# A hybrid encoder step on one core: the b gates formed in the order of the merge, and each output row's sigmoid held behind the last piece of gate a

## The chip, the cores and the metric

The kernel runs on one core of a Trainium2 chip. The metric is the time of one execution on the device in microseconds (us), the median of several runs; lower is better. Beside the runs stands one execution recorded by the hardware profiler. Its views give busy times, waits, transfers and the granted clock of TensorE. In them PE is TensorE, DVE is VectorE, ACT is ScalarE, POOL is GpSimd and SP is SyncE; a q behind the name (SPq, POOLq) is that engine's queue of instructions and DMA issues. "L905" is line 905 of the kernel.

## The reference

One layer of an encoder for 1024 prompt frames and 64 frames of a running stream (1088 in all), D_MODEL = 1024, 8 heads of 64, convolution width 512. Everything is float32. Only the mixer bears on this case:

```python
def mixer(xn, conv_prefix, attn_fn, w_in, w_conv, w_conv_out, w_attn_out, w_out):
    proj = xn @ w_in
    cb, cc, ch, q, k, v, ga, gb = jnp.split(proj, splits, axis=-1)
    cv, conv_state = causal_conv(cc * ch, conv_prefix, w_conv)
    ya = (cb * cv) @ w_conv_out
    o, new_k, new_v = attn_fn(heads(q), heads(k), heads(v))
    yb = o.reshape(B, L, ATT_DIM) @ w_attn_out
    merged = jax.nn.sigmoid(ga) * ya + jax.nn.sigmoid(gb) * yb
    return merged @ w_out, conv_state, new_k, new_v
```

A RMSNorm stands ahead of it, and a residual, a SwiGLU network with a second RMSNorm and a last RMSNorm behind it.

## The kernel before

Arrays lie with channels on the 128 partitions and the 1088 frames along a row, so the 1024 channels of a gate are eight row blocks, m = 0 to 7. A float32 product is made of three matmuls on two-part operands (a rounded "hi" part and the rest, "lo"): `split` writes hi with a cast on ACT (L128) and lo with a subtraction on DVE (L129). A gate's row block is formed by `gate` in four pieces of 272 frames; a piece is 24 matmuls (L343 to L345) into one of three PSUM buffers (`pmm`, `bufs=3`), and what reads the piece out frees the buffer.

Ahead of the part that matters lies the convolution branch, whose result `y_d` (for blocks 0 to 5 already times the sigmoid of gate a) waits in DRAM. Then come ten gate blocks, `GATES`: gate b for m = 0 to 7 as i = 0 to 7, and gate a for m = 6 and 7 as i = 8 and 9. Attention, head after head, is interleaved with them. A piece of gate b is copied out of PSUM by ACT (L908, tile `gst`) and stored by POOL to `gb_d` (L909). A piece of gate a (the last two blocks, `LAST = 2`) is not stored: ACT takes its sigmoid straight out of PSUM into `ga` (L905).

Before gate block 8 attention ends. Its output goes through DRAM: `co` tiles (and `co_s` for the 64 stream frames) are stored to `o_d` by SP (L985, L989), and the reciprocals of the softmax sums (`rows`) are stored to `rc_d` by POOL (L1040, L1044). Heads 0 to 3 come back early (`o0`, `o1`). Those of heads 4 to 7 are read by SP after the last stores: the reciprocals into `rc2` and `rc3` (L1090), and o itself into the tile `ob` (L1170, two loads, called ob k=2 and ob k=3 below). DVE multiplies them (L1172), and `split` writes the pair `ob` (the ACT casts `ob<-o0`, `ob<-o1`, `ob<-rc2`, `ob<-rc3`).

The merge goes over the row blocks in the order `MERGE = [6, 7, 0, 1, 2, 3, 4, 5]`. `rows_in(m)` loads the gate b row from `gb_d` into `z`, named `gb0` to `gb7` (L1138), and the y row into `t`, named `yg0` to `yg7` (L1139); it is called for four blocks before gate block 8 and for the others in the loop. The loop takes z's sigmoid on ACT (L1194), forms `yb` = W_attn_out · o on PE, multiplies by z (L1208), adds to t (L1209) and splits into the operand `mg` of the next product, W_out. `wp10` to `wp17` are the parts of W_attn_out's blocks; their casts and subtractions stand between the others, and their loads (`rawp`, L309) and those of W_out (`wor`, L1233) are issued by POOL.

Each engine works through its own instructions in order; SP's and POOL's DMA issues too. That order is set when the program is built, by a scheduler that orders by data dependences and expected readiness: an instruction that stands late in the source can be placed early on its engine. `tc.issue_after(x)` keeps what is written under it behind instruction x.

Of the kernel before, what the change touches and what calls it, by code (L numbers as in the profile page):

```python
# [10 lines left out]
AF = mybir.ActivationFunctionType  # L11
# [55 lines left out]
def encoder_kernel(ctx: ExitStack, tc: tile.TileContext, ins, outs):  # L67
    nc = tc.nc
    mm = nc.tensor.matmul
    vec, act, pool_e = nc.vector, nc.scalar, nc.gpsimd  # L70
# [55 lines left out]
    def split(hi, lo, src):  # L126

        a = act.copy(hi, src)  # L128
        b = vec.tensor_tensor(lo, src, hi.bitcast(F32), op=ALU.subtract)  # L129
        return a.ins, b.ins  # L130
# [71 lines left out]
    class Unit:  # L202
# [20 lines left out]
        def prep(self, step):  # L223

            a11, a12, a21, a22 = self.block(0, 0), self.block(0, 1), self.block(1, 0), self.block(1, 1)

            def sum(o, x, y, op=ALU.subtract):
                vec.tensor_tensor(o, x, y, op=op)

            if step == 0:  # L230
                self.plain(1, a11)
            elif step == 1:
                self.plain(2, a12)
            elif step == "sums":
                self.s1 = self.temp()
                sum(self.s1, a21, a22, ALU.add)
                self.s2 = self.temp()
                sum(self.s2, self.s1, a11)
                sum(a21, a11, a21)
            elif step == 2:  # L240
                if self.s1 is None:
                    self.prep("sums")
                self.plain(6, self.s2)
            elif step == 3:
                self.plain(7, a21)
            elif step == 4:
                self.plain(5, self.s1)
            elif step == 5:
                self.plain(4, a22)
            else:  # L250
                sum(a12, a12, self.s2)
                self.plain(3, a12)
# [77 lines left out]
    def next_w():  # L330
        i = used[0]
        used[0] += 1
        prep(4 if i == 3 else i + 2)
        return plan[i]

    def product(out, w, x, o, n):

        kt = 4 * len(w)
        for k in range(kt):
            a, b = (t[:, k % 4] for t in w[k // 4])  # L340
            p, q = x.at(0, k, o, n), x.at(1, k, o, n)
            first, then = (q, p) if x is xn and o // HN % 2 == 0 else (p, q)
            mm(out, a, first, start=k == 0, stop=False)  # L343
            mm(out, a, then, start=False, stop=False)  # L344
            newest[0] = mm(out, b, p, start=False, stop=k == kt - 1).ins  # L345

    PIECES = [(j * HN, HN) for j in range(4)]
    GATES = [("b", m) for m in range(8)] + [("a", m) for m in range(6, 8)]
    for g, m in GATES:
        if m % 2 == 0:  # L350
            base = (C_GA if g == "a" else C_GB) + m * P
            ld = {"src": w_in[:, base : base + 2 * P], "w": 2 * P}
        plan.append((ld, KD, m % 2 * P))
    MERGE = [6, 7, 0, 1, 2, 3, 4, 5]
    for m in MERGE[::2]:
        ld = {"src": ins["w_attn_out"][0][:, m * P : (m + 2) * P], "w": 2 * P, "at": 40}
        plan += [(ld, 4, j * P) for j in range(2)]
# [540 lines left out]
    def gate(i, cs):  # L898
        g, m = GATES[i]
        for c in cs:  # L900
            o, n = PIECES[c]
            ps = pmm.tile([P, 512], F32, tag="mm", name=f"g{i}_{c}")
            product(ps[:, :n], gate_w[i], xn, o, n)
            if i >= len(GATES) - LAST:
                act.activation(ga_rows[m - 6][:, o : o + n], ps[:, :n], AF.Sigmoid)  # L905
                continue
            st = st_pool.tile([P, HN], F32, tag="st", name=f"gst{i}_{c}")
            act.copy(st[:, :n], ps[:, :n])  # L908
            nc.gpsimd.dma_start(gb_d[m * P : (m + 1) * P, o : o + n], st[:, :n])  # L909

    gate_w = {}

    heads, sums = {}, {}

# [169 lines left out]
    def row_tile(l, nm):  # L1084
        return qp.tile([P, T], F32, tag=f"q{l}", name=nm, bufs=2 + l)
# [42 lines left out]
    def between():  # L1128
        credit[0] += PER
        while credit[0] >= 1:  # L1130
            credit[0] -= 1
            next(steps, None)
# [3 lines left out]
    def rows_in(m):  # L1136
        t, z = rows[m] = u_rows.tile([P, T], F32, tag="yg", name=f"yg{m}"), row_tile((MERGE.index(m) % 5 + 1) % 2, f"gb{m}")
        nc.sync.dma_start(z, gb_d[m * P : (m + 1) * P])  # L1138
        nc.sync.dma_start(t, y_d[m * P : (m + 1) * P])  # L1139
# [4 lines left out]
    for i in range(4):  # L1144
        gate_w[i] = next_w()
        gate(i, (0, 1))
    for i in range(4):
        for c in (2, 3):
            gate(i, (c,))
            between()  # L1150
        if i == 0:
            prep(5)
    for i in range(4, len(GATES)):
        gate_w[i] = next_w()
        if i == len(GATES) - LAST:
            for _ in steps:
                pass
            att_stack.close()
            uo = pg_stack.enter_context(tc.tile_pool(name="uo", bufs=1, reuse_waits="tile"))
            uo.tile([P, 48], F32, name="pad_ob")  # L1160
            t = uo.tile([P, 2, 4 * T + 8], F32R, name="ob")[:, :, : 4 * T]
            ob = Acts(t.rearrange("p l (k t) -> p l k t", k=4))
            u_rows = pg_stack.enter_context(tc.tile_pool(name="u_rows", bufs=5, reuse_waits="tile"))
            ga_rows = [uo.tile([P, T], F32, name=f"ga{m}") for m in (6, 7)]
            for k in range(2):
                split(ob.t[:, 0, k], ob.t[:, 1, k], o_rows[k])
            late_r = row_tile(1, "rc2"), row_tile(0, "rc3")
            for k, r in zip((2, 3), late_r):
                o = ob.t[:, 0, k].bitcast(F32)
                nc.sync.dma_start(o, o_d[k * P : (k + 1) * P])  # L1170
                rc_load(r, k)
                vec.tensor_tensor(r, o, r, op=ALU.mult)  # L1172
                split(ob.t[:, 0, k], ob.t[:, 1, k], r)
            for m in MERGE[:4]:
                rows_in(m)
        for c in range(4):
            gate(i, (c,))
            between()
        if i >= len(GATES) - LAST:
            m = GATES[i][1]  # L1180
            t = rows[m][0]
            vec.tensor_tensor(t, t, ga_rows[m - 6], op=ALU.mult)
# [5 lines left out]
    psum2 = pg_stack.enter_context(tc.tile_pool(name="psum2", bufs=2, space=PSUM, reuse_waits="tile"))  # L1188
    for n, m in enumerate(MERGE):
        wb = next_w()  # L1190
        if n + 4 < 8:
            rows_in(MERGE[n + 4])
        t, z = rows.pop(m)
        act.activation(z, z, AF.Sigmoid)  # L1194
        late = t.rearrange("p (h n) -> p h n", h=2)[:, :, 512:]
        hi, lo = (ms[:, m, l].rearrange("p (h n) -> p h n", h=2) for l in range(2))
        for h in range(2):
            yb = psum2.tile([P, 2, 512], F32, tag="mm", name=f"yb{m}_{h}")
            for j in range(2):
                if n == 0:  # L1200
                    with tc.issue_after(gates_end):
                        product(yb[:, j, :HN], wb, ob, h * HT + j * HN, HN)
                else:
                    product(yb[:, j, :HN], wb, ob, h * HT + j * HN, HN)
            hs = slice(h * HT, (h + 1) * HT)
            zh, th = z[:, hs], t[:, hs]
            two = zh.rearrange("p (j n) -> p j n", j=2)
            vec.tensor_tensor(two, yb[:, :, :HN], two, op=ALU.mult)  # L1208
            vec.tensor_tensor(th, th, zh, op=ALU.add)  # L1209
            split(mg.at(0, m, h * HT, HT), mg.at(1, m, h * HT, HT), th)  # L1210
        pool_e.tensor_copy(hi, late)
        pool_e.tensor_tensor(lo, late, hi.bitcast(F32), op=ALU.subtract)
# [13 lines left out]
    def bank2(tag, nm):  # L1226
        return psA.tile([P, 2, 512], F32, tag=tag, name=nm, bufs=2)
# [50 lines left out]
    if True:  # L1278
# [5 lines left out]
        for i in (0, 1, 2, 3, 8, 4, 5, 6, 7):  # L1284
            t0, n = TT[i]
            xt = wp.tile([P, D], F32, tag="xg", name=f"xr{i}")[:, :512]
            nc.sync.dma_start(xt[:n], x_rows(i)[:, :512])
            ps = bank2("BD", f"wo0_{i}")[:, 0]
# [373 lines left out]
    for n in range(1, len(names)):  # L1662
# [7 lines left out]
        if 2 <= n < 18:  # L1670
            nm, src = (("k", ck), ("v", cvv))[(n - 2) // 8]
            a = (n - 2) % 8 * 56
# [58 lines left out]
    for b, ks in enumerate(blocks):  # L1731
        first, final = b == 0, b == len(blocks) - 1
        nk = blocks[b + 1] if not final else []
        for g in range(2):
            ps = {}
# [27 lines left out]
            for si, js in turns:  # L1763
                p, ht = STEPS[si], hts[base + si]
                key = {1: "A", 6: "A", 5: "A", 3: "A", 2: "B", 7: "D", 4: "D"}[p]
                for j in js:
# [20 lines left out]
                    o = acc[i + 4 * h, d]  # L1787
# [7 lines left out]
                    if final and si == 2:  # L1795
                        for hh, dd in ((0, 0), (1, 1), (1, 0), (0, 1)):
                            a = acc[i + 4 * hh, dd]
# [71 lines left out]
```

## Time and profile before

| | us |
|---|---|
| median of 3 runs | 1467.02 |
| lowest and highest run | 1465.70, 1467.43 |
| the profiled execution, its time | 1467.9 |
| the profiled execution, its span from the first to the last instruction | 1466.1 |
| PE busy (share of the span) | 1449.1 (99%) |
| DVE, ACT, POOL busy | 993.3, 679.7, 154.4 |
| mean granted clock of TensorE | 0.997 |

The profiled execution took 0.9 us longer than the median. Its times are counted from its first instruction. The gates and attention fill 387 to 616 us of it, the merge 616 to 669 us. A row of the timeline gives start, duration, engine, line, operation, out<-in, shapes and count, and in brackets the idle time of the engine just before with what ended it. Matmuls overlap in the pipeline, so what one costs is read from start to start.

### The profile page before, as it was taken

Reading aid. Unit: us, or ns where it says so; the run is one execution under the profiler, and the core shown is the slowest. Engines: PE = TensorE matmul, PEld = TensorE weight load, DVE = VectorE, ACT = ScalarE, POOL = GpSimd, SP = SyncE. Lnnn points to the kernel's source line nnn. Section 1 sums busy time; section 2 is a strip of 40 time slices with the busy share of each in tenths; the row PEclk is TensorE's granted clock in tenths of the full one; section 3 lists DMA queues with packets and bytes.
Section 4 is the critical chain, followed back from the end, with each engine's and each line's share of the span. In section 5 each row is a group of like instructions: output and inputs, shape, how many; then the busy total and the mean of one; then the engine's idle time right before and its main releaser. Section 6 shows DMA issues by size and latency. Waiting matters only on the chain.

```text
span 1466.1 us, 26257 instructions
## 1 busy us (share of the span) xinstructions
PE 1449.1 (99%) x10137; PEld 1362.2 (93%) x10137; DVE 993.3 (68%) x1831; ACT 679.7 (46%) x1354; POOL 154.4 (11%) x282
## 2 busy tenths in 40 slices
PE   8999999999999999999999999999999999999997
PEld 6899999999999989998889999999999998888886
DVE  7975565658357767473588667766666668957676
ACT  7644343336367667431355444444344445512223
POOL 1400010001221121111100111111011111000000
PEclk9999999999999999999999999999999999999999
DMA  8687612235877675743432444443334449877685
GB/s 286 182 276 226 197 56 71 67 111 200 261 214 195 177 189 150 260 149 126 156 108 80 160 162 157 151 168 129 122 130 169 148 179 313 274 232 249 210 266 204
DMA packets 156221, 262.47 MB, mean 179 GB/s; under 512 B 18529, under 2 KB 89377, under 8 KB 156097
## 3 DMA queue, kind: packets, MB, share of 16 engines
q1 hardware_dynamic: 132336, 184.33, 40.0%
q0 software_dynamic: 22608, 74.38, 14.2%
q10 hardware_dynamic: 1152, 2.10, 0.4%
q8 instruction: 79, 1.29, 0.4%
q14 instruction: 46, 0.37, 0.1%
HBM read 171.78 MB, written 90.81 MB: 179 GB/s over the span
## 4 chain that ended last, share of the span: by engine, by line
PE 92%; DVE 4%; DMA 2%; ACT 2%; issue 1%; ACTq 0%; SPq 0%; DVEq 0%
PE Ab L277 8%; PE Aa L277 8%; PE A L1779 7%; PE Da L277 4%; PE Db L277 4%; PE D L1779 3%; PE g L344 3%; PE g L345 3%; PE g L343 3%; PE Aga L277 2%; PE Ba L277 2%; PE Bb L277 2%; PE wo L1251 2%; PE wo L1253 2%; PE wo L1252 2%; PE B L1779 2%
## 5 line engine op out<-in xcount | busy, mean ns | idle before, releaser
L343 PE MATMUL g<-xn,wp 128*128 128x272 f32 x320 | 94.9, 297 | 2.3 <-ACT ga L905 2.3
L344 PE MATMUL g<-xn,wp 128*128 128x272 f32 x320 | 93.9, 293 | 0.0
L345 PE MATMUL g<-xn,low 128*128 128x272 f32 x320 | 93.7, 293 | 0.0
L128 ACT CAST ring<-w2r 128x512 fp32r<-128x512 f32 (+1 forms) x78 | 43.2, 588 | 98.8 <-PE A L1779 50.7
L964 DVE CUSTOM_DVE_ANT_0 p<-s,bb 128x640 f32<-128x640 f32 (+5 forms) x72 | 47.6, 662 | 38.9 <-PE s L1007 37.2
L1779 PE MATMUL A<-ring,ht 128*128 128x512 f32 (+1 forms) x267 | 72.5, 387 | 0.3 <-ACT acc L1792 0.3
L1779 PE MATMUL A<-ring,low 128*128 128x512 f32 (+1 forms) x270 | 72.6, 385 | 0.0
L129 DVE TENSOR_TENSOR low<-rawa,wa 128x512 fp32r<-128x512 f32 x55 | 37.7, 687 | 42.0 <-ACT wa L128 42.0
L343 PEld LDWEIGHTS g<-xn,wp 128*128 128x128 f32 x320 | 61.1, 191 | 3.1 <-ACT ga L905 2.5
L344 PEld LDWEIGHTS g<-xn,wp 128*128 128x128 f32 x320 | 61.1, 191 | 0.5
L345 PEld LDWEIGHTS g<-xn,low 128*128 128x128 f32 x320 | 61.0, 191 | 0.4
L1779 PEld LDWEIGHTS A<-ring,ht 128*128 128x128 f32 x267 | 49.7, 188 | 10.7 <-ACT acc L1792 0.7
L1779 PEld LDWEIGHTS A<-ring,low 128*128 128x128 f32 x270 | 50.2, 188 | 10.2
L129 DVE TENSOR_TENSOR ring<-w2r,ring 128x512 fp32r<-128x512 f32 (+1 forms) x78 | 49.1, 647 | 14.1 <-ACT ring L128 14.1
L277 PE MATMUL Ab<-tt,wb 128*128 128x272 f32 x352 | 57.8, 286 | 0.4 <-ACT wb L128 0.4
L277 PE MATMUL Ab<-mg,wb 128*128 128x272 f32 x352 | 58.0, 286 | 0.0
L277 PE MATMUL Aa<-mg,wa 128*128 128x272 f32 x352 | 57.7, 285 | 0.0
L277 PE MATMUL Aa<-tt,wa 128*128 128x272 f32 x352 | 57.7, 285 | 0.0
L974 ACT ACTIVATE p<-p,mx 128x640 f32<-128x640 f32 (+5 forms) x72 | 50.8, 706 | 13.7 <-DVE mx L964 13.2
L128 ACT CAST wa<-rawa 128x512 fp32r<-128x512 f32 x55 | 34.0, 621 | 47.4 <-PE Ab L277 33.3
L129 DVE TENSOR_TENSOR pt<-t,pt 128x640 fp32r<-128x640 f32 (+2 forms) x64 | 41.8, 653 | 15.6 <-ACT pt L128 14.7
L128 ACT CAST wb<-rawb 128x512 fp32r<-128x512 f32 x55 | 34.0, 620 | 38.4 <-PE Aa L277 24.2
(591 smaller groups left out, 4507.8 us busy)
## 6 DMA issues: line engine op xcount, KB each, us to landing
h_d<-hq POOLq DMA_DIRECT2D x44, 512.0 KB, 3.9
ht<-h_d SPq DMA_DIRECT2D x77, 256.0 KB, 3.6
low<-h_d SPq DMA_DIRECT2D x77, 256.0 KB, 4.2
h_d<-hq_early POOLq DMA_DIRECT2D x29, 512.0 KB, 4.2
rawa<-in_w_ff SPq DMA_DIRECT2D x11, 1024.0 KB, 5.6
rawb<-in_w_ff SPq DMA_DIRECT2D x11, 1024.0 KB, 5.3
w2r<-in_w_ff SPq DMA_DIRECT2D x11, 1024.0 KB, 8.1
qd<-q_d SPq DMA_DIRECT2D x32, 272.0 KB, 4.2
```

The lines of the kernel that those rows point to most:

```text
L128: a = act.copy(hi, src)
L129: b = vec.tensor_tensor(lo, src, hi.bitcast(F32), op=ALU.subtract)
L277: newest[0] = mm(t[:, j, :HN], w[:, k, :], x[p][:, k, l, j * HN : (j + 1) * HN], start=p in (1, 2, 7) and k == 0 and n == 0, stop=k == las ...
L343: mm(out, a, first, start=k == 0, stop=False)
L344: mm(out, a, then, start=False, stop=False)
L345: newest[0] = mm(out, b, p, start=False, stop=k == kt - 1).ins
L964: vec.tensor_tensor_reduce(out=s if len(ps.shape) == 2 else s.rearrange("p (a b) -> p a b", a=2), in0=ps, in1=bias if len(ps.shape) == 2 e ...
L974: act.activation(s, s, AF.Exp, bias=mx, scale=-1.0, accum_out=sm)
L1251: mm(ps, x(k, 0), wh, start=f, stop=False)
L1252: mm(ps, x(k, 1), wh, start=False, stop=False)
L1253: mm(ps, x(k, 0), wl, start=False, stop=e)
L1779: mm(t[:, c], ht[k][:, j, x], w[:, l, c], start=p in (1, 2, 7) and k == 0 and n == 0, stop=k == len(ks) - 1 and n == 2, skip_group_check=p ...
```

## The change

The gate b blocks are formed in the order of `MERGE`, so gate blocks i = 0 to 7 are now m = 6, 7, 0, 1, 2, 3, 4, 5. The sigmoid of z in the merge loop may not be placed ahead of the newest sigmoid of gate a, which at that point of the source is the last piece of block 9. Lines behind L1193 move by one. No instruction is added or taken away on any engine.

```diff
     PIECES = [(j * HN, HN) for j in range(4)]
-    GATES = [("b", m) for m in range(8)] + [("a", m) for m in range(6, 8)]
+    MERGE = [6, 7, 0, 1, 2, 3, 4, 5]
+    GATES = [("b", m) for m in MERGE] + [("a", m) for m in range(6, 8)]
     ...
-    MERGE = [6, 7, 0, 1, 2, 3, 4, 5]
     ...
             if i >= len(GATES) - LAST:
-                act.activation(ga_rows[m - 6][:, o : o + n], ps[:, :n], AF.Sigmoid)
+                gate_out[0] = act.activation(ga_rows[m - 6][:, o : o + n], ps[:, :n], AF.Sigmoid).ins
                 continue
     ...
-    gate_w = {}
+    gate_w, gate_out = {}, [None]
     ...
         t, z = rows.pop(m)
-        act.activation(z, z, AF.Sigmoid)
+        with tc.issue_after(gate_out[0]):
+            act.activation(z, z, AF.Sigmoid)
```

On PE, DVE and POOL the instructions stand in the same order as before, with the same tiles, except that the pieces of gate b belong to other m. On two engines the order changes.

ACT at the end of attention, before: `ca7_s` is the last copy of attention, `ga6` the sigmoid of gate block 8 (pieces g8_0 to g8_3), `ga7` that of block 9.

```order
L980 COPY ca7_s_7063<-pv7_8_7057 64x64
L1194 ACT_TABLE_LOAD
L1194 ACTIVATE gb7_7113<-gb7_7113 128x1088
L128 CAST ob_7084<-o0_6819 128x1088
L128 CAST ob_7084<-o1_6862 128x1088
L905 ACTIVATE ga6_7088<-g8_0_7124 128x272
L905 ACTIVATE ga6_7088<-g8_1_7150 128x272
L905 ACTIVATE ga6_7088<-g8_2_7176 128x272
L128 CAST wp14_0_7555<-rawp14_7415 128x512
L128 CAST ob_7084<-rc2_7094 128x1088
L905 ACTIVATE ga6_7088<-g8_3_7202 128x272
L128 CAST wp15_0_7623<-rawp14_7415 128x512
```

The same place now:

```order
L980 COPY ca7_s_7063<-pv7_8_7057 64x64
L128 CAST ob_7084<-o0_6819 128x1088
L128 CAST ob_7084<-o1_6862 128x1088
L905 ACT_TABLE_LOAD
L905 ACTIVATE ga6_7088<-g8_0_7124 128x272
L905 ACTIVATE ga6_7088<-g8_1_7150 128x272
L905 ACTIVATE ga6_7088<-g8_2_7176 128x272
L128 CAST ob_7084<-rc2_7094 128x1088
L128 CAST wp14_0_7555<-rawp14_7415 128x512
L128 CAST ob_7084<-rc3_7095 128x1088
L905 ACTIVATE ga6_7088<-g8_3_7202 128x272
L128 CAST wp15_0_7623<-rawp14_7415 128x512
```

The sigmoid of gb7 has left the head of this stretch, and the cast `ob<-rc3`, which stood behind `wp15`, now stands ahead of the sigmoid of piece g8_3.

ACT a little later, at the end of the gates, before: `mg` is the merged operand.

```order
L128 CAST ob_7084<-rc3_7095 128x1088
L1194 ACTIVATE gb6_7109<-gb6_7109 128x1088
L905 ACTIVATE ga7_7089<-g9_0_7234 128x272
L905 ACTIVATE ga7_7089<-g9_1_7260 128x272
L1194 ACTIVATE gb0_7117<-gb0_7117 128x1088
L905 ACTIVATE ga7_7089<-g9_2_7286 128x272
L1194 ACTIVATE gb1_7121<-gb1_7121 128x1088
L128 CAST wp16_0_7687<-rawp16_7553 128x512
L128 CAST wp17_0_7751<-rawp16_7553 128x512
L905 ACTIVATE ga7_7089<-g9_3_7312 128x272
L1194 ACTIVATE gb2_7351<-gb2_7351 128x1088
L128 CAST mg10_7340<-yg6_7108 128x544
```

And now:

```order
L905 ACTIVATE ga7_7089<-g9_0_7234 128x272
L905 ACTIVATE ga7_7089<-g9_1_7260 128x272
L905 ACTIVATE ga7_7089<-g9_2_7286 128x272
L128 CAST wp16_0_7687<-rawp16_7553 128x512
L128 CAST wp17_0_7751<-rawp16_7553 128x512
L905 ACTIVATE ga7_7089<-g9_3_7312 128x272
L1195 ACTIVATE gb6_7109<-gb6_7109 128x1088
L1195 ACTIVATE gb7_7113<-gb7_7113 128x1088
L1195 ACTIVATE gb0_7117<-gb0_7117 128x1088
L1195 ACTIVATE gb1_7121<-gb1_7121 128x1088
L128 CAST mg10_7340<-yg6_7108 128x544
L1195 ACTIVATE gb2_7351<-gb2_7351 128x1088
```

The four sigmoids of the rows that are loaded first now stand in one block behind the last piece of gate a.

SP's queue at the end of attention, before:

```order
L1090 DMA rc2_7094<-rc_d_93 64x1088 x2
L985 DMA o_d_92<-co7_2_6983 64x256
L1138 DMA gb7_7113<-gb_d_91 128x1088
L985 DMA o_d_92<-co7_3_7052 64x256
L1090 DMA rc3_7095<-rc_d_93 64x1088
L989 DMA o_d_92<-co7_s_7064 64x32 x2
L1170 DMA ob_7084<-o_d_92 128x1088 x2
L1138 DMA gb6_7109<-gb_d_91 128x1088
```

And now:

```order
L1090 DMA rc2_7094<-rc_d_93 64x1088 x2
L1138 DMA gb7_7113<-gb_d_91 128x1088
L985 DMA o_d_92<-co7_2_6983 64x256
L985 DMA o_d_92<-co7_3_7052 64x256
L1090 DMA rc3_7095<-rc_d_93 64x1088
L989 DMA o_d_92<-co7_s_7064 64x32 x2
L1170 DMA ob_7084<-o_d_92 128x1088 x2
L1138 DMA gb6_7109<-gb_d_91 128x1088
```

The load of gb7 has moved ahead of the store of `co7_2`. It no longer waits for the stores of gate block 7, since block m = 7 is now formed as i = 1.

## The prediction

> **What bounds the kernel now.** I read the page first, its busy times and chain: PE is busy for 99% of the span, so a change is worth what it does to PE's few idle stretches or to PE's clock.
>
> ```profile
> PE 1449.1 (99%) x10137; PEld 1362.2 (93%) x10137; DVE 993.3 (68%) x1831; ACT 679.7 (46%) x1354; POOL 154.4 (11%) x282
> PE 92%; DVE 4%; DMA 2%; ACT 2%; issue 1%; ACTq 0%; SPq 0%; DVEq 0%
> ```
>
> Next the waits of PE from 560 to 760 us, around the change, and the same stretch cut at that wait (columns: time, busy us of each engine, PEclk, DMA share, GB/s).
>
> ```profile
> PE g L343 <- ACT ga L905: 2.3, 1, 2.3
> 597.20:600.10 2.90, 0.62 (x5) 0.43 (x4) 1.87 (x2) 2.88 (x6) 0.00 (x0) 1.00 0.70 135
> 600.10:603.50 3.40, 3.40 (x17) 3.40 (x16) 1.76 (x2) 0.72 (x2) 0.00 (x0) 0.50 0.83 259
> 603.50:616.30 12.80, 12.80 (x105) 12.80 (x104) 6.96 (x8) 5.99 (x9) 1.59 (x2) 1.00 0.97 371
> 616.30:666.00 49.70, 49.70 (x394) 49.41 (x393) 36.78 (x54) 19.93 (x31) 6.91 (x16) 1.00 0.50 172
> ```
>
> PE stalls once, for ACT's sigmoid of a gate piece, and then runs 3.4 us at half the granted clock. The whole merge behind it (last row) has PE busy without a gap. PE's own rows at the stall (first matmul of piece g8_2, its last; first of g8_3; first of g9_0; last of g9_3):
>
> ```profile
> 594.24 0.29 PE L343 MATMUL g<-xn,wp 128*128 128x272 f32 x1
> 597.11 0.29 PE L345 MATMUL g<-xn,low 128*128 128x272 f32 x1
> 599.67 0.39 PE L343 MATMUL g<-xn,wp 128*128 128x272 f32 x1 [2.27 <-ACT ga L905]
> 604.32 0.29 PE L343 MATMUL g<-xn,wp 128*128 128x272 f32 x1
> 616.17 0.29 PE L345 MATMUL g<-xn,low 128*128 128x272 f32 x1
> ```
>
> From 604.32 to 616.17 lie 95 steps, 0.125 us each, so a piece costs 24 x 0.125 = 3.0 us and block 9 ends its issue at 616.3. Piece g8_3 could have begun at 597.11 + 0.13 = 597.24. It lost 599.67 - 597.24 = 2.43 us to the stall, and 604.32 - 599.67 - 3.0 = 1.65 us to the half clock: 4.08 us together.
>
> Why ACT was late, in its timeline:
>
> ```profile
> 591.24 0.21 ACT L980 COPY ca_s<-pv 64x64 f32<-64x64 f32 x1 [1.92 <-PE pv L1065]
> 594.80 1.28 ACT L1194 ACT_TABLE_LOAD   x1 [3.35 <-DMA gb<-gb_d]
> 596.10 1.11 ACT L1194 ACTIVATE gb<-gb 128x1088 f32<-128x1088 f32 x1
> 597.12 2.08 ACT L128 CAST ob<-o 128x1088 fp32r<-128x1088 f32 x2
> 599.22 0.98 ACT L905 ACTIVATE ga<-g 128x272 f32<-128x272 f32 x3
> 603.69 1.10 ACT L128 CAST ob<-rc 128x1088 fp32r<-128x1088 f32 x1 [0.83 <-DVE rc L1172]
> 604.70 0.39 ACT L905 ACTIVATE ga<-g 128x272 f32<-128x272 f32 x1
> 608.44 1.11 ACT L128 CAST ob<-rc 128x1088 fp32r<-128x1088 f32 x1 [2.84 <-DVE rc L1172]
> ```
>
> ACT sat 3.35 us in front of gb7's sigmoid, with the two `ob` casts and the sigmoid of g8_0, whose PSUM buffer g8_3 needs, queued behind it.
>
> **The stall that goes.** With gb7's sigmoid gone from there, the casts start behind `ca_s` at 591.45 and take 2.08 us. They need o0 and o1, which DVE finished long before (row below), and nothing that comes later. Then the table load, 1.28, which moves in front of the first gate a sigmoid: 594.8; g8_0 is released at 595.2. That is 2 us ahead of PE's wish at 597.24. Gain: 4.08 us. Pieces g8_3, g9_0 and g9_1 then run from 597.24 to 606.24; g9_0 and g9_1 need the sigmoids of g8_1 and g8_2, whose inputs end at about 594.5 and 597.5 and which nothing precedes.
>
> ```profile
> 577.83 1.28 DVE L1104 TENSOR_TENSOR o<-o,rc 128x1088 f32<-128x1088 f32 x1
> ```
>
> **The stall that comes.** Piece g9_2 needs the buffer of g8_3, so g8_3's sigmoid. In the new order that stands behind `ob<-rc3`, which in the profile ran only at 608.44 because DVE's product waited for the load ob k=3:
>
> ```profile
> 602.37 1.29 DVE L1172 TENSOR_TENSOR rc<-ob,rc 128x1088 f32<-128x1088 f32 x1 [1.64 <-DMA ob<-o_d]
> 607.11 1.29 DVE L1172 TENSOR_TENSOR rc<-ob,rc 128x1088 f32<-128x1088 f32 x1 [2.85 <-DMA ob<-o_d]
> ```
>
> From the landing at 607.1 the old rows give: ACT's cast 1.33 us after DVE's start, ACT's next instruction 1.01 later, the sigmoid 0.39, PE 0.06 behind it. So PE resumes about 2.8 us after that landing. If it stays at 607.1, PE resumes at 609.9 where it wished 606.24, and a stall of 3.66 us replaces one of 2.43. What the change is worth hangs on the landing of ob k=3.
>
> **What moves that landing.** SP's queue, POOL's last store of `rc_d`, and the transfers issued from 588 to 591 us (KB, median us to landing), with those of the head before, 566 to 569:
>
> ```profile
> 581.86 1.15 SPq L1090 DMA_DIRECT2D rc<-rc_d  x2
> 589.57 0.33 SPq L1138 DMA_DIRECT2D gb<-gb_d  x1
> 590.25 0.46 SPq L985 DMA_DIRECT2D o_d<-co  x1
> 596.23 0.46 SPq L1090 DMA_DIRECT2D rc<-rc_d  x1
> 596.79 1.18 SPq L989 DMA_DIRECT2D o_d<-co_s  x2
> 598.13 2.51 SPq L1170 DMA_DIRECT2D ob<-o_d  x2
> 589.84 0.51 POOL L1044 DMA_DIRECT2D rc_d<-rows  x1
> ```
>
> ```profile
> gb<-gb_d SPq DMA_DIRECT2D x1, 544.0 KB, 5.1
> o_d<-co SPq DMA_DIRECT2D x1, 64.0 KB, 6.0
> rc_d<-rows POOLq DMA_DIRECT2D x2, 0.1 KB, 6.2
> ...
> rc_d<-rows POOLq DMA_DIRECT2D x2, 0.1 KB, 3.2
> ```
>
> SP stood from 590.7 to 596.23 for the last `rc_d` store: 589.84 + 6.2 = 596.1. The same store of the head before landed in 3.2 us. Between them lies the load of gb7, 544 KB issued at 589.57, just ahead. Now it is issued behind the `rc2` loads, at 583.05, and at its 5.1 us lands by 588.2, before the last `rc_d` store is on its way. It is put ahead of one store on SP (`co7_2`, ready at about 586), where 0.33 us of issue is covered, since SP waits there anyway; the 544 KB may hold that store, a POOL weight load and gate b's last piece back by a microsecond or two, and nobody needs these before 592. So I take 3.2 us: the last `rc_d` store lands at 593.0, 3.1 earlier. Behind it SP's chain is in order and unchanged: `rc3` load, `co_s` stores, ob k=2, then ob k=3 as soon as `co_s` has landed, and `co_s` is ready (DVE formed it at 592). The ob k=3 load took 6.8 us with the loads of gb and yg rows close behind it, and they move with it:
>
> ```profile
> ob<-o_d SPq DMA_DIRECT2D x1, 544.0 KB, 6.8
> ```
>
> So it lands at 607.1 - 3.1 = 604.0, and PE resumes at 604.0 + 2.8 = 606.8, a new stall of 0.57 us. Bounds: no shift (3.66 us of stall, and the half clock again, 1.65, as the shorter idle of 2.43 brought it), and no stall if it lands by 603.4, which is beyond the shift that the 3.2 us row allows.
>
> **The sum.** 4.08 gained, 0.57 lost: 3.5 us. Block 9 ends at 612.8 instead of 616.3. Against the profiled execution's 1467.9 that makes 1464.4; it stood 0.9 above the median, and against the median of 1467.02 it makes 1463.5, or 1463.6 with about 0.1 for the pipeline's restart behind the new stall.
>
> **The held sigmoids cost nothing.** They run 4 x 1.02 us (596.10 to 597.12 above) behind g9_3's sigmoid. That needs g9_3's end, 0.3 behind the last issue, and its 0.39, so gb6 is ready 1.8 us after block 9's end. DVE's first product needs yb6's first half, 3.3 us after it; in the old run it came 4.3 us after it:
>
> ```profile
> 619.37 1.28 DVE L1182 TENSOR_TENSOR yg<-yg,ga 128x1088 f32<-128x1088 f32 x1
> 620.58 0.72 DVE L1208 TENSOR_TENSOR gb<-yb,gb 128x544 f32<-128x544 f32 x1
> 622.09 0.65 ACT L128 CAST mg<-yg 128x544 fp32r<-128x544 f32 x1 [1.45 <-DVE yg L1209]
> ```
>
> The cast of `mg` wants to start 3.3 + 1.44 = 4.7 us after block 9 and ACT is free at 0.7 + 4.1 = 4.8. PE needs the first half's buffer only 6 us after it. Cover: yb's two halves in PSUM. If DVE were over 2 us late there, PE would stall. The reordered b blocks are the same 24-matmul pieces with equal weight loads, and the row formed last, m = 5, is loaded last: nothing.
>
> **Rivals.**
> 1. *The stall only moves (slower than before).* If the `rc_d` store is slow whoever stands before it, the landing stays at 607.1: +4.08 - 3.66 - 1.65 = -1.23 us, 1468.2. For it: gb7's load now runs right behind the `rc2` loads of 581.86 and may still be moving when the store is issued. Against: the 3.2 us row. It decides when the landing moves by less than about 1.2 us with the half clock.
> 2. *Half the shift.* Landing near 605.5: stall 2.1 us, with or without the half clock: 1465.0 to 1466.7.
> 3. *The half clock isn't in the median.* A stall of 2.4 us brings half clock only where the throttle's judging lets it; in another execution it may not. Then the gain is 2.43 - 0.57 = 1.86 us, 1465.2. For it: the runs differ by 1.73 us (1465.70 to 1467.43), about the 1.65. Against: two of the three lie high, as the profiled one does, and that one had the 0.50 row.
>
> The Trainium skill ("TensorE: Matmul & The Clock Gate", the section on HAM oscillation) gives the rule that idle gaps over about 3.4 us throttle PE. The trace disagrees: 2.43 us did. By that rule the half clock would not follow from this stall, and the time would come out as in rival 3.
>
> **How the numbers follow.** Forecast 0.50, its own range 1462.8 to 1464.3; rival 1 0.12; rival 2 0.15; rival 3 0.18; anything else 0.05. Predicted is 1463.6. Eight times in ten takes in rivals 2 and 3 up to 1466.9 and leaves out rival 1: 1462.7 to 1466.9. A measurement here tells 0.2% (2.9 us) from no change, so faster means under 1464.1: nearly all of the forecast, 0.47. Same, 0.48: the rest of it and all three rivals. Slower, over 1470, needs rival 1 with a later landing still: 0.05.
>
> **What would show it.** In the new profile: ACT's `ob` casts directly behind `ca_s` near 591.5; no wait of PE at g8_3; the gb7 load near 583 and SP's `rc3` load near 593 instead of 596.2; ob k=3 landing near 604; a PE wait of about 0.6 us on the sigmoid of g8_3, at full clock; the merge without a PE gap. It is wrong if SP's `rc3` load stays near 596, if a second half-clock stretch appears near 610, or if PE waits in the merge.

## The result and the profile after

The changed kernel takes 1464.03 us in the median (17 runs, 1462.82 to 1467.10). The kernel before, run beside it, takes 1467.18 (17 runs, 1465.27 to 1470.57). The ratio is 0.9980, with a 95% interval of 0.9973 to 0.9986, so 3.15 us were gained. The profiled execution took 1463.09 us, with a span of 1460.5.

From the page of the changed kernel, the busy times and the chain that ended last:

```profile
PE 1446.7 (99%) x10137; PEld 1360.4 (93%) x10137; DVE 994.5 (68%) x1831; ACT 679.8 (47%) x1354; POOL 154.4 (11%) x282
PE 95%; DVE 3%; ACT 1%; issue 0%; DMA 0%; SPq 0%; ACTq 0%; DVEq 0%
```

PE does the same 10137 matmuls in 2.4 us less, of which the half clock makes about 1.7 (3.4 us at 0.50), and the chain goes through PE for 95% instead of 92%: the 2% that it spent in DMA are gone. The wait of PE that is left between 560 and 760 us:

```profile
PE t L1053 <- DVE pt L129: 0.2, 1, 0.2
```

It lies in attention. The wait on ACT's gate sigmoid is gone, and none has come in its place. The stretch in windows (columns as in the prediction): first the two that held the stall and the half clock, then all from the last attention product (590.9 before, 589.9 now) to the first `yb` product, and from there to the first `wo` product, with the same two cuts of the kernel before between them:

```profile
597.20:600.10 2.90, 2.90 (x25) 2.90 (x25) 1.90 (x2) 1.36 (x2) 0.21 (x1) 1.00 0.97 365
600.10:603.50 3.40, 3.40 (x29) 3.40 (x28) 2.25 (x2) 1.19 (x2) 0.60 (x1) 1.00 1.02 413
```

```profile
590.90:616.30 25.40, 23.12 (x171) 22.84 (x171) 11.02 (x12) 12.18 (x18) 1.59 (x2) 0.93 0.77 260
616.30:664.40 48.10, 48.10 (x387) 48.10 (x386) 35.89 (x53) 18.85 (x28) 6.91 (x16) 1.00 0.52 177
```

```profile
589.90:611.20 21.30, 21.30 (x170) 21.20 (x170) 11.71 (x13) 9.92 (x16) 1.59 (x2) 1.00 0.85 294
611.20:659.30 48.10, 48.10 (x386) 48.10 (x385) 35.44 (x52) 21.23 (x30) 6.91 (x16) 1.00 0.51 174
```

The gates behind attention took 25.40 us and take 21.30, at full clock and without a gap. The merge takes 48.10 in both. So the stage became 4.1 us shorter, and the whole of it came from the place where the stall was. The two profiled spans differ by 5.6 us. Of the other 1.5 us, the new run was 1.0 ahead already when the last attention product began (589.9 against 590.9), and 0.5 fell behind the first `wo` product, where the order of work is the same.

ACT in the changed kernel, from the end of attention to the first cast of the merged operand:

```profile
590.29 0.21 ACT L980 COPY ca_s<-pv 64x64 f32<-64x64 f32 x1 [1.93 <-PE pv L1065]
590.60 2.10 ACT L128 CAST ob<-o 128x1088 fp32r<-128x1088 f32 x2
592.73 1.28 ACT L905 ACT_TABLE_LOAD   x1
594.02 0.69 ACT L905 ACTIVATE ga<-g 128x272 f32<-128x272 f32 x2
...
602.58 1.10 ACT L128 CAST ob<-rc 128x1088 fp32r<-128x1088 f32 x1 [2.21 <-DVE rc L1172]
603.58 0.39 ACT L905 ACTIVATE ga<-g 128x272 f32<-128x272 f32 x1
...
611.85 0.39 ACT L905 ACTIVATE ga<-g 128x272 f32<-128x272 f32 x1
612.14 4.10 ACT L1195 ACTIVATE gb<-gb 128x1088 f32<-128x1088 f32 x4
616.14 0.64 ACT L128 CAST mg<-yg 128x544 fp32r<-128x544 f32 x1
```

The casts follow `ca_s` at once, where ACT sat 3.35 us before. The sigmoid of g8_3 (603.58) ends at 603.97, 1.3 us before PE wants its buffer. The four held sigmoids run in one piece of 4.10 us and the cast of `mg` follows without idle time.

SP's queue and the DMA issues of POOL's last stores (KB, median us to landing), with the loads of `ob`:

```profile
582.09 0.58 SPq L1138 DMA_DIRECT2D gb<-gb_d  x1
590.86 0.46 SPq L1090 DMA_DIRECT2D rc<-rc_d  x1
592.77 2.90 SPq L1170 DMA_DIRECT2D ob<-o_d  x2
```

```profile
rc_d<-rows POOLq DMA_DIRECT2D x2, 0.1 KB, 1.8
ob<-o_d SPq DMA_DIRECT2D x1, 544.0 KB, 5.9
```

The load of gb7 is issued at 582.09, behind the `rc2` loads. The small stores then land in 1.8 us instead of 6.2, SP loads `rc3` at 590.86 instead of 596.23, and DVE's product for ob k=3 starts at 601.25 instead of 607.11:

```profile
601.25 1.29 DVE L1172 TENSOR_TENSOR rc<-ob,rc 128x1088 f32<-128x1088 f32 x1 [1.95 <-DMA ob<-o_d]
614.53 0.72 DVE L1209 TENSOR_TENSOR gb<-yb,gb 128x544 f32<-128x544 f32 x1 [0.67 <-PE yb L345]
```

### The profile page after: what moved, and what is told of

It is laid out like the page before. It is cut to its first block, busy times and chain, and to the rows that moved or that the text cites. A ratio compares the mean times of both kernels' runs of the same rounds, so it can differ in the third digit from the quotient of the medians.

```text
span 1460.5 us, 26260 instructions
## 1 busy us (share of the span) xinstructions
PE 1446.7 (99%) x10137; PEld 1360.4 (93%) x10137; DVE 994.5 (68%) x1831; ACT 679.8 (47%) x1354; POOL 154.4 (11%) x282
## 4 chain that ended last, share of the span: by engine, by line
PE 95%; DVE 3%; ACT 1%; issue 0%; DMA 0%; SPq 0%; ACTq 0%; DVEq 0%
PE Ab L277 9%; PE Aa L277 8%; PE A L1780 8%; PE Db L277 4%; PE Da L277 4%; PE D L1780 4%; PE g L344 3%; PE g L345 3%; PE g L343 3%; PE Aga L277 2%; PE B L1780 2%; PE Bb L277 2%; PE Ba L277 2%; PE wo L1252 2%; PE wo L1254 2%; PE wo L1253 2%
```

## The experiments

The theory: the whole gain comes from the place of gb7's load on SP. At its old place this 544 KB transfer does two things: it lands late itself, and ACT waits for it; and it holds up the last `rc_d` store, with it `rc3`, ob k=3 and the cast `ob<-rc3`. The hold on the sigmoids takes away only the first, and so moves the stall from g8_3 to g9_2. The rivals: the hold on ACT is what counts, or the two are needed together; and for the size of the gain, that the half clock is in only some of the executions of the kernel before. The diffs are against the changed kernel. One quantity is read from each profile: the stage from the start of the last attention product (`pv`, L1065) to the start of the first `wo` product on PE. Before it is 664.4 - 590.9 = 73.5 us, in the changed kernel 659.3 - 589.9 = 69.4.

**The hold alone.** The gate blocks in the order of before:

```diff
-    GATES = [("b", m) for m in MERGE] + [("a", m) for m in range(6, 8)]
+    GATES = [("b", m) for m in range(8)] + [("a", m) for m in range(6, 8)]
```

> The hold alone: gate b formed in the old order 0 to 7, each row's sigmoid held behind the last piece of gate a. ACT then has the new order, with the cast ob<-rc3 ahead of the sigmoid of piece g8_3, and SP the old one, with the load of gb7 between the stores of co7_2 and co7_3. Theory (the gain needs both: ACT free, and the last rc_d store not behind the gb7 load): PE's wait at g8_3 goes, the last rc_d store still takes about 6 us to land, ob k=3 lands near 607, and PE waits 3 to 4 us at g9_2 with a half-clock stretch behind it; time 1466 to 1469, the same as the kernel before or up to 1.5 us slower. Rival (the hold on ACT is all that counts): no PE wait over 0.5 us, about 1464.

Measured: 1466.06 us (12 runs, 1464.14 to 1470.56) against 1468.15 (18 runs), ratio 0.9991 with an interval of 0.9980 to 1.0003. The stage takes 71.2 us. Its profile, SP first, then ACT, then PE's wait:

```profile
589.79 0.33 SPq L1138 DMA_DIRECT2D gb<-gb_d  x1
596.10 0.46 SPq L1090 DMA_DIRECT2D rc<-rc_d  x1
```

```profile
591.54 0.21 ACT L980 COPY ca_s<-pv 64x64 f32<-64x64 f32 x1 [1.92 <-PE pv L1065]
591.86 2.11 ACT L128 CAST ob<-o 128x1088 fp32r<-128x1088 f32 x2
...
606.72 1.10 ACT L128 CAST ob<-rc 128x1088 fp32r<-128x1088 f32 x1 [1.91 <-DVE rc L1172]
607.72 0.39 ACT L905 ACTIVATE ga<-g 128x272 f32<-128x272 f32 x1
```

```profile
608.17 0.39 PE L343 MATMUL g<-xn,wp 128*128 128x272 f32 x1 [1.48 <-ACT ga L905]
```

The hold does what it says (the casts come right behind `ca_s`, and g8_3 starts on time), but gb7's load still stands at 589.79, `rc3` is loaded as late as before, and the stall turns up at g9_2. This is the prediction's rival 1, at its place. Its size was overestimated: I had put ob k=3 near its old landing of 607, and it came at 605.4, so 1.48 us of stall at full clock and not 3 to 4. Two more profiles of the same kernel:

> The hold alone, a second profile. Its runs fell into two groups, 1464.1 to 1466.6 and 1469.0 to 1470.6 us, and the profile (span 1464.4) belongs to the first: a stall of 1.5 us at g9_2, full clock. Theory: the second group is the moved stall at its full size, with ob k=3 landing near 607, a PE wait of 3 us or more at g9_2 and half a clock behind it; a profile of that group shows these, and one of the first group shows 1 to 2 us at full clock. Rival: the second group loses its time elsewhere (in the merge or before the gates), and PE's wait at g9_2 is the same in both.

> The hold alone, a third profile. Theory: 1 to 2 us of PE wait at g9_2 at full clock in a run of the fast group, 3 us or more and a half-clock stretch in one of the slow group. Rival: the same wait in both groups.

They took 1469.67 and 1465.08 us beside one run of before at 1467.92, with stages of 73.6 and 70.3 us. PE's wait at g9_2 in the first, then in the second:

```profile
609.35 0.39 PE L343 MATMUL g<-xn,wp 128*128 128x272 f32 x1 [2.37 <-ACT ga L905]
609.80:613.20 3.40, 3.40 (x18) 3.40 (x17) 2.27 (x2) 0.59 (x3) 0.00 (x0) 0.51 0.96 351
```

```profile
607.31 0.39 PE L343 MATMUL g<-xn,wp 128*128 128x272 f32 x1 [0.40 <-ACT ga L905]
609.80:613.20 3.40, 3.40 (x30) 3.40 (x29) 1.13 (x3) 1.02 (x2) 0.78 (x1) 1.00 1.02 395
```

So the hold alone gives anything from nothing (2.37 us of stall and then the half clock) to 3 us (0.40 us of stall), as the landing falls: DVE's product for ob k=3 starts at 606.57 in the first of these two and at 604.53 in the second, against 605.39 in the profile above. The half clock came as I expected it for the slower runs, but the stall there was 2.37 us and not 3 or more; in the faster one it was below the 1 to 2 us expected. Its runs spread over 6.4 us (those of before over 5.9, those of the next two kernels over 1.5 and 2.0), and whether its median gains is unclear.

**The order alone.** The sigmoid without the hold:

```diff
-        with tc.issue_after(gate_out[0]):
-            act.activation(z, z, AF.Sigmoid)
+        act.activation(z, z, AF.Sigmoid)
```

> The order alone: gate b formed in the order of the merge, no hold. SP then has the new order (gb7 loaded behind rc2), ACT has gb7's sigmoid with its table load ahead of the copy ca7_s, and the cast ob<-rc3 behind the sigmoid of g8_3 as in the kernel before. Theory: gb7 has landed long before ACT comes to its sigmoid, so ACT waits for no load there; the 2.3 us of table load and sigmoid fit nearly into the 1.9 us that ACT idles before ca7_s; no PE wait over 0.3 us; the whole gain without the hold, 1463.5 to 1464.5. Rival (the hold is needed, since ACT still takes a sigmoid ahead of the ob casts): a PE wait at g8_3 of 1 us or more, 1465 or more.

Measured: 1463.63 us (5 runs, 1462.74 to 1464.25) against the same 1468.15, ratio 0.9968 (0.9955 to 0.9981); the stage takes 69.4 us, and PE has no wait in it but the 0.2 of attention. ACT:

```profile
590.54 1.11 ACT L1194 ACTIVATE gb<-gb 128x1088 f32<-128x1088 f32 x1
591.55 0.19 ACT L980 COPY ca_s<-pv 64x64 f32<-64x64 f32 x1
591.65 2.10 ACT L128 CAST ob<-o 128x1088 fp32r<-128x1088 f32 x2
```

A sigmoid of a gb row still stands at the head of this stretch, but its row is there, so, counted from the last attention product, `ca_s` comes only about 0.5 us later than in the changed kernel and the casts about 0.3. The order alone gives the whole 4.1 us. DVE's merge starts 3.22 us behind the first `yb` product, against 3.28 in the changed kernel.

**The hold, with gb7's load late.** The gate blocks in the order of before, the sigmoids held, and the load of gb7 kept on SP behind the two loads of `ob`:

```diff
-                nc.sync.dma_start(o, o_d[k * P : (k + 1) * P])
+                ob_in[0] = nc.sync.dma_start(o, o_d[k * P : (k + 1) * P]).ins
     ...
-        nc.sync.dma_start(z, gb_d[m * P : (m + 1) * P])
+        if m == 7:
+            with tc.issue_after(ob_in[0]):
+                nc.sync.dma_start(z, gb_d[m * P : (m + 1) * P])
+        else:
+            nc.sync.dma_start(z, gb_d[m * P : (m + 1) * P])
```

> As the hold alone, but the load of gb7 is held behind the two ob loads on SP, so it no longer stands ahead of the last rc_d store, though gate b is formed in the old order. Theory: the last rc_d store lands in 2 to 3 us instead of 6, ob k=3 lands 3 to 5 us earlier than with the hold alone, no PE wait over 0.6 us at g9_2; 1463.5 to 1464.5. Rival (the landing of ob k=3 depends on something else than the gb7 load): as the hold alone, 1466 to 1469, with a PE wait at g9_2.

Measured: 1464.22 us (6 runs, 1463.59 to 1465.54) against the same 1468.15, ratio 0.9972 (0.9961 to 0.9983), stage 69.4 us. SP, then ACT:

```profile
591.48 0.46 SPq L1090 DMA_DIRECT2D rc<-rc_d  x1
593.39 3.66 SPq L1174 DMA_DIRECT2D ob<-o_d  x2
598.13 0.36 SPq L1140 DMA_DIRECT2D gb<-gb_d  x1
```

```profile
602.63 1.10 ACT L128 CAST ob<-rc 128x1088 fp32r<-128x1088 f32 x1 [1.48 <-DVE rc L1176]
603.64 0.39 ACT L905 ACTIVATE ga<-g 128x272 f32<-128x272 f32 x1
```

The gates are formed in the order of before, and the whole gain is there all the same: `rc3` is loaded at 591.48 and the sigmoid of g8_3 runs at 603.64, within 0.7 us of the changed kernel's times. The trace has no landing for the small store itself, but SP goes on to `rc3` 1.64 us behind its issue (589.84); in the kernel before that took 6.39 us. In the two traces ACT, DVE and POOL work in the same order from attention's end into the merge, and on SP only the load of gb7 stands elsewhere: the place of the 544 KB load among the transfers alone tells this kernel from the hold alone. So the order of the gates acts by making gb7 ready early enough to be loaded ahead of the attention's last stores. Moving the load behind them instead does as well together with the hold. Without the hold a sigmoid would wait for it at the head of ACT's stretch; that kernel was not run.

**The kernel before, three more times,** for the half clock:

> The kernel before once more, for its clock. Theory (the stall of 2.4 us at g8_3 brings half a clock in some executions only, so the median's gain is less than the 4.1 us of the profiled execution): the stall stands in every profile, the half-clock stretch of 3.4 us behind it in some. Rival: the half clock is there every time.

> The kernel before, a third profile. In the first the stall at g8_3 (2.3 us) brought half a clock for 3.4 us; in the second a stall of 2.0 us brought none, and PE lost 0.8 us more to a late DVE in the merge. Theory: the stall at g8_3 is there each time, between 1.9 and 2.6 us; the half clock and the wait in the merge come and go. Rival: one of the three is the rule and the other profile was an exception, so that two more profiles look alike.

> The kernel before, a fourth profile. Theory: the stall at g8_3 stands again, 1.9 to 2.6 us; half clock and merge wait come and go. Rival: it looks like the third in every point.

They took 1468.3, 1468.7 and 1468.03 us, with the same span of 1466.1 each and stages of 73.3, 73.4 and 73.7 us. PE's wait at g8_3 and the 3.4 us behind it, in the first and the second:

```profile
600.07 0.39 PE L343 MATMUL g<-xn,wp 128*128 128x272 f32 x1 [1.95 <-ACT ga L905]
600.50:603.90 3.40, 3.40 (x29) 3.40 (x28) 2.52 (x3) 1.37 (x3) 0.00 (x0) 1.00 0.89 291
```

```profile
600.20 0.39 PE L343 MATMUL g<-xn,wp 128*128 128x272 f32 x1 [2.25 <-ACT ga L905]
600.50:603.90 3.40, 3.40 (x17) 3.40 (x16) 2.52 (x3) 1.26 (x3) 0.00 (x0) 0.50 0.90 303
```

The third waited 2.46 us and had the half clock too. The first had none, and lost time elsewhere instead: its merge took 49.8 us and not 48.1. There PE waited 0.81 us, which the other profiles of before do not have, for DVE, which waited for ACT, which waited 1.30 us for a gb row that was still loading:

```profile
634.15 0.39 PE L343 MATMUL yb<-ob,wp 128*128 128x272 f32 x1 [0.81 <-DVE gb L1208]
629.04 1.11 ACT L1194 ACTIVATE gb<-gb 128x1088 f32<-128x1088 f32 x1 [1.30 <-DMA gb<-gb_d]
```

**The change and the order alone, side by side on another chip:**

> The changed kernel again, on one chip with the order alone. Theory: from attention's last product to the first product with W_out it takes 69.4 us, as in its first profile and as with the order alone, 4.1 us less than the kernel before; the gain on this chip is 3 to 4.6 us. Rival: the hold is worth something of its own, and it is faster or slower than the order alone by over 0.8 us.

> The order alone again, beside the changed kernel. Theory: the same time within 0.5 us, since neither has a PE wait at the gates; DVE starts the merge about a microsecond later after the gates than with the hold, because sigmoids of gb rows stand ahead of g9_3's, and that is covered by yb's two buffers. Rival: that later start turns into PE waits in the merge in some executions, and its runs spread further than with the hold.

They took 1464.02 us (11 runs, 1463.22 to 1465.44) and 1464.59 (11 runs, 1463.07 to 1465.35) against 1466.35 (21 runs, 1463.29 to 1469.22): ratios 0.9985 (0.9976 to 0.9994) and 0.9986 (0.9977 to 0.9995), and stages of 69.4 us both. The hold adds nothing to the order that these runs can tell. DVE's merge in the order alone starts 3.22 us behind the first `yb` product again, and not the microsecond later that I had expected. The gain in the median is 2.3 and 1.8 us and not the 3 to 4.6 that I had expected, at the same stage time: the kernel before was faster on this chip, and why is open.

Each run also records its mean granted clock. Of the 39 runs of before in the two timed comparisons, 16 had 0.997 or less, the value of the first profile; of the 33 runs of the changed kernel, the order alone and the hold with the late load, none had. In the second comparison the 9 runs of before at 0.997 have a median of 1467.16, the 12 others 1465.75; in the first the 7 have 1468.36, the 11 others 1467.71. A run at 0.998 can still hold a half-clock stretch (the hold's 1469.67 us did), and every profile also ends with 3.0 to 5.9 us at half clock behind PE's last matmul, which count in the mean. So this is a hint and no clean cut.

## Why the prediction was right, and where it was off

- *The stall that goes*, 4.08 us: right. The stage became 4.1 us shorter in every profile in which the transfers stand in the new order or the late one (five profiles, 69.4 each).
- *What moves that landing*: the cause was right, and the late load shows it by itself. The size was low. I took 3.2 us for the last `rc_d` store and it took 1.8 (2.2 in the order alone, 2.6 in the repeat of the change). The row of the head before, from which I took the 3.2, was no undisturbed one: there too SP had issued a 544 KB load, 2.5 us ahead of that store. From the kernel before:

```profile
565.68 0.72 SPq L1102 DMA_DIRECT2D o<-o_d  x1
o<-o_d SPq DMA_DIRECT2D x1, 544.0 KB, 4.9
```

It landed at 570.6, and the store, issued at 568.1, at 571.3. I took 6.8 for ob k=3, and 5.9 was measured; the 6.8 is the longest of the four profiles of before (6.8, 6.2, 4.3 and 4.4). I had expected `rc3` at 593.0 and the landing at 604.0; they came at 590.86 and 601.2, of which the earlier start of the run makes 1.0. So the landing came, by the clock of before, at 602.2, ahead of the 603.4 that I had held to be out of reach.

- *The stall that comes*, 0.57 us: this term was mis-sized, by the two landing times above. It is 0, since the sigmoid of g8_3 runs well ahead of PE's wish. So the profile gained 4.1 where the sum said 3.5. The mechanism was shown in the hold alone, where the landing does stay late and PE does wait at g9_2.
- *The held sigmoids cost nothing*: right. DVE's merge starts 3.28 us behind the first `yb` product (3.3 forecast), and the merge keeps its 48.10 us.
- *Rival 3*, the half clock that isn't in the median: partly true. The sum counted the half clock in full, and one of four profiles of before lacks it, its wait there being 1.95 us; 23 of 39 runs show a mean clock that does not ask for it. It is one reason why the median gained 3.15 us (in the other comparisons of a kernel without the stall 1.8 to 4.5) and the profile's stage 4.1. That the forecast of 1463.6 came so close to the measured 1464.03 is therefore partly luck: a gain counted 0.6 too small in the stage stands against a median that holds the stall's full price in some executions only.
- *Rival 1* did not happen with the order changed, and happened in part without it.

Two things stay open. The fastest two runs of before (1463.29 and 1463.49 us) come close to the changed kernel, and neither has a profile; whether the stall was gone there is not known. And the small store took 1.8 us in one profile of the change and 2.6 in the other. In the slower one POOL's four small stores landed one behind the other from 591.57 to 592.08, right behind the 136 KB store of gate b ahead of them on the same queue (585.88, 5.5 us to landing); in the faster one that store had landed at 589.3. Why it took longer there is open.

## What to carry to other kernels

A wait of the busiest engine can be caused by a big transfer that nobody needs yet: here a row that DVE's merge used only after 616 us, loaded at 589.57, just ahead of a small store on which a chain of loads hung. With the hold alone no engine waited for that row, and PE stalled all the same. Before moving work on the engine that waits, follow its input back through the queues to the first transfer that is slower than its like elsewhere in the trace, and look at what was issued just ahead of it; moving that one to either side was enough here (to the late side together with the hold). And before taking a transfer's time as the undisturbed one, look at what was in flight ahead of it as well. Holding back an instruction without moving its transfer only handed the stall to the next user of the same buffer.

## What the runs showed of the hardware

The small store. The last 0.1 KB stored by POOL's queue landed in 1.8 to 2.6 us when the load of gb7 was issued early, and in 5.7 to 6.5 us in the profiles of before and of the hold alone that tell it, where the load was issued 0.25 to 0.6 us ahead. From the two repeats of the hold alone (the second first; gb7's load in both took 5.4 us):

```profile
rc_d<-rows POOLq DMA_DIRECT2D x2, 0.1 KB, 5.7
```

```profile
rc_d<-rows POOLq DMA_DIRECT2D x2, 0.1 KB, 6.5
```

The first profile of the hold alone has both cases side by side: of its two 0.1 KB stores, one was issued at 589.13, ahead of the load (589.79), and landed in 1.6 us; the other, issued at 590.14, behind it, took 5.8:

```profile
DMA to landing us min/median/max: 1.6/3.7/5.8
```

So a store issued just behind the load lands only 0.8 to 1.5 us after the load does, although the two are issued by different engines.

The clock. PE's waits of 2.25, 2.27, 2.37 and 2.46 us were each followed by 3.4 us at half the granted clock, and those of 0.40, 1.48 and 1.95 us by none: the price of this stall jumps by about 1.7 us somewhere between 1.95 and 2.25. In the third repeat of before, whose wait of 2.46 us ended at 600.17, the half clock came only about 1.3 us later:

```profile
600.20:601.30 1.10, 1.10 (x9) 1.10 (x10) 1.02 (x1) 0.50 (x2) 0.00 (x0) 1.00 0.70 261
601.50:604.80 3.30, 3.30 (x17) 3.30 (x16) 1.89 (x2) 1.48 (x2) 0.00 (x0) 0.50 0.88 305
```

The Trainium skill ("TensorE: Matmul & The Clock Gate", the section on HAM oscillation) puts the limit for idle gaps at about 3.4 us. These runs disagree: a wait of 2.25 us, a third shorter, was followed by the half clock.
